# Hyena filter stage: last layer's weights as sum and difference, channel sums as columns with a small reciprocal, absolute sum as a maximum, one written order

## The chip, the core and the metric

The kernel runs on one core of a Trainium2 chip. The core has TensorE (PE, matrix products into PSUM), VectorE (DVE), ScalarE (ACT), GpSimd (POOL) and DMA queues that are issued by SyncE (SP). Each engine takes its instructions in one order and waits at semaphores for the others. The metric is the device time of one execution in microseconds; the time of a kernel is the median of its runs.

## The reference

Two blocks of a diffusion transformer work on 512 image tokens and 256 context tokens of width 1024. The first block's mixer is half a Fourier transform and half a Hyena operator: a convolution as long as the sequence, whose filter comes from a small network over positions. This is the part that the change rewrites:

```python
h = jnp.sin(f * (h @ w3 + b3))          # third sine layer
h = h @ w4                              # L x 1024
h_fwd = h[:, :512] * decay
h_bwd = h[:, 512:] * decay
two_sided = concatenate([h_fwd, zeros((1, 512)), h_bwd[:0:-1]])
two_sided = two_sided / sum(abs(two_sided), axis=0)
return rfft(two_sided, axis=0)
...
u_h = dwconv3(proj[..., 512:], conv_w, conv_b)
x0, x1, v = split(u_h, 3)
y_h = x0 * long_conv(v * x1, spectrum, hy_bias)
```

The first time step of h_bwd is left out of the filter (in its place stands the row of zeros). The division is by one absolute sum for each of the 512 channels. The filter is made for the image (512 steps) and for the context (256 steps).

## The kernel before

Products in this kernel are made of three: each fp32 operand is split into a rounded high half and the remainder, its low half, and high by high, low by high and high by low are added in PSUM (L149, L150, L151). For a weight this means a load of 512 KB into a buffer `wr`, the high half `wh` on ScalarE (L124) and the low half `wl` on VectorE (L129). There are three buffers each of `wr`, `wh` and `wl`, in rotation, and the rows of the modulation weights (`wmodT`, two products with `junk` at L241 on VectorE) pass through `wr` too. In the text such a row with its two products is a modulation row, and its products a modulation pair.

PSUM has three buffers `mm` of 1024 columns and two `ms` of 512. A result must leave its `mm` buffer before the third next product may start.

The mixer starts with the norm and projections 0 to 2, for which an order of PE, DVE, ACT and SP is written out by hand. With them run three sine layers of the filter's network; the last sine (L382 to L391 on VectorE, then L412 on ScalarE) makes `h3`. Then the filter stage follows, between about 72 and 156 us of the profile. In it:

- Six time tiles of 128 steps (4 and 5 for the context, 0 to 3 for the image): `filter_mm` (L421) makes forward and backward halves as a product of `h3` with `w4`. `filter_pm` multiplies both with the decay on VectorE (L430, L431), clears the first time step of the backward half, makes sum and difference on GpSimd (L437), their high halves on ScalarE, and the absolute sum of both halves with two ScalarE operations and one on GpSimd (L441 to L443). `filter_lo` makes the low halves.
- `filter_sum` (L459): the sum over time as a product with a 128 x 128 block of constants, so that each partition holds all 512 sums, and a reciprocal of 128 x 512 on VectorE (L461).
- `filter_spec`: a Fourier table `ftab` times the tiles, 12 products for each of the context's two tables, 24 for each of the image's four. `filter_scale` (L497 to L499) multiplies with the reciprocal and adds the skip row `brow`. `filter_nyquist` (L475 to L478) makes the one row of the highest frequency.
- Between them lie projections 3, 4 and 5. The last two go through `conv3`: one ScalarE operation (L371) and two on VectorE (L372, L373), which read the projection's PSUM buffer.

Behind the stage come projections 12, 8, 13, 9, 14, 10, 15 and 11 with their convolutions, folds and transposes (L695). In the filter stage and behind it the order on every engine is chosen by a scheduler, with the edges that `issue_after` adds.

Of the kernel before, what the change touches and what calls it, by code (L numbers as in the profile page):

```python
# [76 lines left out]
class Builder:  # L77
# [117 lines left out]

    def load_sb(self):
        nc = self.nc
        for j in range(2):
            nc.sync.dma_start(self.sb[:, j, :], self.I["cboth"][j : j + 1, :].partition_broadcast(P))
            nc.scalar.activation(self.sb[:, j, :], self.sb[:, j, :], AF.Silu)  # L200
# [223 lines left out]

    def filter_pm(self, ps, dec, first):

        nc, v = self.nc, self.nc.vector
        f = self.t(self.S2, [P, 512], F32, "s2")
        b = self.t(self.S2, [P, 512], F32, "s2")
        v.tensor_tensor(f, ps[:, 0:512], dec, op=ALU.mult)  # L430
        v.tensor_tensor(b, ps[:, 512:1024], dec, op=ALU.mult)  # L431
        if first:
            v.memset(b[0:1, :], 0.0)
        parts = []
        for tg, op in (("ap", ALU.add), ("am", ALU.subtract)):
            s = self.t(self.S2, [P, 512], F32, "s2")
            nc.gpsimd.tensor_tensor(s, f, b, op=op)  # L437
            hi = self.t(self.pg, [P, 512], F32R, tg + "h", 4)
            self.hi(hi, s)
            parts.append((s, hi))  # L440
        nc.scalar.activation(f, f, AF.Abs)  # L441
        nc.scalar.activation(b, b, AF.Abs)
        nc.gpsimd.tensor_tensor(f, f, b, op=ALU.add)  # L443
        return parts, f

    def filter_lo(self, parts):
        out = []
        for tg, (s, hi) in zip(("ap", "am"), parts):
            lo = self.t(self.pg, [P, 512], F32R, tg + "l", 4)
            self.lo(lo, s, hi)  # L450
            out.append((hi, lo))
        return out

    def filter_sum(self, sums, nhalf):

        ps = self.ms()
        on = self.onesN[nhalf]
        for i, f in enumerate(sums):
            self.nc.tensor.matmul(ps, on, f, start=i == 0, stop=i == len(sums) - 1)  # L459
        S = self.t(self.pf, [P, 512], F32, "S")  # L460
        self.nc.vector.reciprocal(S, ps)  # L461
        return S
# [45 lines left out]
    def mixer(self):  # L508
# [9 lines left out]
        for nh in (512.0, 256.0):  # L518
            self.onesN[nh] = self.t(self.pf, [P, P], F32, f"on{int(nh)}")
            v.memset(self.onesN[nh], nh)  # L520
# [1315 lines left out]
```

## Time and profile before

| | us |
|---|---|
| median of 3 runs | 1661.32 |
| lowest and highest run | 1657.84 and 1666.68 |
| the profiled execution | 1657.69 |
| its span, first to last instruction | 1655.9 |
| VectorE busy from 72 to 160 us with low halves of weights (L129, 12 of 128 x 1024 or 512) | 17.0 |
| VectorE busy there with modulation products (L241, 13) | 16.8 |
| VectorE busy there with the two wide reciprocals (L461) | 6.7 |

A line of a group in the profile names a line of the program, an engine, an operation, the tiles (out<-in) and a shape, then busy time, the mean of one and the idle time before it with what ended that. In a timeline the columns are the start in us, the duration, the engine, the line and the tiles; in brackets stands how long the engine sat idle before it, and who released it. Of stretches of the run (from:to) the busy time of each engine is given, in the order PE, weight loads (PEld), DVE, ACT, POOL, then the clock that was granted to TensorE (1.00 is full speed), the share of DMA and GB/s. The duration of a matmul overlaps the next one; its cost is from start to start.

### The profile page before, as it was taken

What the parts mean: (1) busy time and instruction counts of PE and PEld (TensorE: products, weight loads), DVE (VectorE), ACT (ScalarE), POOL (GpSimd) and SP (SyncE); (2) the same over time, 40 slices, a digit from 0 to 9 for tenths busy, and PEclk for the clock granted to TensorE, in tenths of its full rate; (3) what the DMA queues carried; (4) which work ended last, traced back from release to release, by engine and by line L of the source; (5) the groups of instructions that cost most, each with busy time, mean ns of one, the idle gap of its engine ahead of it and who ended that gap; (6) DMA issues with size and microseconds to landing.
All of it is one profiled execution on the core that took longest, in us unless ns stands there. A gap on an engine that the chain in (4) does not pass through costs nothing.

```text
span 1655.9 us, 20680 instructions
## 1 busy us (share of the span) xinstructions
PE 1588.1 (96%) x8178; PEld 1290.3 (78%) x8178; DVE 1057.4 (64%) x1695; ACT 617.4 (37%) x876; POOL 125.7 (8%) x177
## 2 busy tenths in 40 slices
PE   4989998999999999999998999999999999999999
PEld 2757787888888888888887887666659878878877
DVE  5698969967877354553444576899987544344243
ACT  4432224424222112222122245989864433133131
POOL 0152115000000000000000000222210000000000
PEclk9999999999999999999999999999999999999999
DMA  9325411432444133431430420000014222222222
GB/s 345 132 77 179 173 61 61 170 137 98 156 153 153 64 127 141 142 139 64 140 115 30 146 68 20 13 10 13 1 69 166 85 97 94 90 101 90 89 89 89
DMA packets 54540, 173.34 MB, mean 105 GB/s; under 512 B 6187, under 2 KB 9453, under 8 KB 53421
## 3 DMA queue, kind: packets, MB, share of 16 engines
q1 hardware_dynamic: 54445, 172.03, 29.3%
q8 instruction: 64, 1.05, 0.2%
q14 instruction: 31, 0.25, 0.0%
HBM read 166.24 MB, written 5.77 MB: 104 GB/s over the span
## 4 chain that ended last, share of the span: by engine, by line
PE 77%; DVE 14%; DMA 3%; POOL 2%; ACT 2%; issue 2%; SPq 0%; POOLq 0%; DVEq 0%; ACTq 0%
PE mm L149 23%; PE mm L151 23%; PE mm L150 23%; PE pv L1506 2%; DVE junk L241 2%; DVE wl L129 1%; DVE S L1482 1%; PE s L1452 1%; DMA wr<-wmodT 1%; POOL s L437 1%; DVE wr L1521 1%; PE k L149 1%; PE k L151 1%; PE k L150 1%; DVE mx L1466 0%
## 5 line engine op out<-in xcount | busy, mean ns | idle before, releaser
L149 PE MATMUL mm<-hh,wh 128*128 128x512 f32 (+2 forms) x1360 | 482.5, 358 | 10.6 <-DVE x L373 6.6
L151 PE MATMUL mm<-hh,wl 128*128 128x512 f32 (+2 forms) x1360 | 480.2, 354 | 1.6 <-DVE wl L129 1.6
L150 PE MATMUL mm<-hl,wh 128*128 128x512 f32 (+2 forms) x1360 | 480.3, 354 | 1.4 <-DVE hl L311 1.4
L124 ACT ACTIVATE wh<-wr 128x1024 fp32r<-128x1024 f32 (+2 forms) x192 | 197.6, 1032 | 584.5 <-PE mm L150 554.5
L129 DVE TENSOR_TENSOR wl<-wr,wh 128x1024 fp32r<-128x1024 f32 (+2 forms) x192 | 233.9, 1221 | 254.8 <-ACT wh L124 248.3
L149 PEld LDWEIGHTS mm<-hh,wh 128*128 128x128 f32 x1360 | 257.6, 190 | 58.8 <-issue 14.5
L150 PEld LDWEIGHTS mm<-hl,wh 128*128 128x128 f32 x1360 | 257.9, 190 | 39.5 <-DVE hl L311 2.5
L151 PEld LDWEIGHTS mm<-hh,wl 128*128 128x128 f32 x1360 | 258.0, 190 | 38.4 <-DVE wl L129 1.8
L241 DVE SCALAR_TENSOR_TENSOR junk<-wr,sb 128x1024 bf16<-128x1024 f32 x128 | 157.3, 1229 | 29.8 <-DMA wr<-wmodT 28.8
L151 PE MATMUL mm<-ah,wl 128*128 128x512 f32 (+1 forms) x480 | 172.3, 359 | 0.0
L150 PE MATMUL mm<-al,wh 128*128 128x512 f32 (+1 forms) x480 | 172.1, 359 | 0.0
L149 PE MATMUL mm<-ah,wh 128*128 128x512 f32 (+1 forms) x480 | 172.1, 359 | 0.0
L1048 DVE SCALAR_TENSOR_TENSOR xr<-mm,mod,xr 128x512 f32<-128x512 f32 (+1 forms) x100 | 61.8, 632 | 153.1 <-PE mm L151 152.7
L149 PEld LDWEIGHTS mm<-ah,wh 128*128 128x128 f32 x480 | 90.4, 188 | 14.7 <-issue 0.2
L150 PEld LDWEIGHTS mm<-al,wh 128*128 128x128 f32 x480 | 90.3, 188 | 14.6
L151 PEld LDWEIGHTS mm<-ah,wl 128*128 128x128 f32 x480 | 90.2, 188 | 14.4
L1506 PE MATMUL pv<-S,V 128*128 128x512 f32 x192 | 93.8, 597 | 2.6 <-ACT S L1485 2.6
L1072 ACT ACTIVATE fg<-fg 128x772 f32<-128x772 f32 (+1 forms) x44 | 32.6, 741 | 98.3 <-DVE fg L373 98.3
L1460 ACT ACTIVATE S<-s,rks 128x512 f32<-128x512 f32 x96 | 62.8, 686 | 12.0 <-PE pv L1506 8.0
L1506 PEld LDWEIGHTS pv<-S,V 128*128 128x128 f32 x192 | 34.4, 190 | 34.9 <-issue 29.4
L1478 POOL PARTITION_ALL_REDUCE mx<-mx x16 | 45.2, 2825 | 162.8 <-DVE mx L1475 162.8
L1482 DVE TENSOR_TENSOR S<-S,mx 128x1536 f32<-128x1536 f32 x32 | 55.3, 1749 | 2.3 <-POOL mx L1478 2.3
(330 smaller groups left out, 2266.1 us busy)
## 6 DMA issues: line engine op xcount, KB each, us to landing
wr<-w_up SPq DMA_DIRECT2D x88, 512.0 KB, 3.2
wr<-wmodT SPq DMA_DIRECT2D x80, 512.0 KB, 3.2
wr<-w_dn SPq DMA_DIRECT2D x32, 512.0 KB, 3.2
wm<-wmod0a SPq DMA_DIRECT2D x8, 1024.0 KB, 7.8
wr<-w_in SPq DMA_DIRECT2D x16, 512.0 KB, 3.2
wr<-w_out SPq DMA_DIRECT2D x13, 512.0 KB, 3.2
wr<-w_dn SPq DMA_DIRECT2D x17, 384.0 KB, 3.3
wr<-w_o SPq DMA_DIRECT2D x11, 512.0 KB, 3.2
```

Source lines behind the costliest of these rows:

```text
L124: self.nc.scalar.activation(dst, src, AF.Copy)
L129: (eng or self.nc.vector).tensor_tensor(dst, src, hi.bitcast(F32), op=ALU.subtract)
L149: mmul(out, wh, xh, start=start, stop=False)
L150: mmul(out, wh, xl, start=False, stop=False)
L151: mmul(out, wl, xh, start=False, stop=stop)
L241: nc.vector.scalar_tensor_tensor(junk, raw, 1.0, self.sb[:, j, :], op0=ALU.mult, op1=ALU.mult, accum_out=acc)
L1048: nc.vector.scalar_tensor_tensor(x[m][:, a2:b2], ps[:, a2:b2], mod[:, 8 * sec + m, c : c + 1], x[m][:, a2:b2], op0=ALU.mult, op1=ALU.add)
L1072: nc.scalar.activation(g[:, :n], g[:, :n], AF.Silu)
L1460: nc.scalar.activation(c.S[a][j // 3][:, j % 3, :], c.ps[a, j], AF.Copy, scale=c.r[:, g : g + 1])
L1478: nc.gpsimd.partition_all_reduce(c.m[a][:, 1, :], c.m[a][:, 0, :], P, bass.bass_isa.ReduceOp.max)
L1482: v.tensor_tensor(c.S[a][h], c.S[a][h], mb.to_broadcast([P, 3, T]), op=ALU.subtract)
L1506: nc.tensor.matmul(c.P[a], V[:, j, o : o + 128], c.S[a][j // 3][:, j % 3, :], start=j == 0, stop=j == 5)
```

## The change

The stage computes the same filter with other steps, and a written order takes the place of the scheduler's.

- `filter_w4` (new): the halves of `w4` are replaced by their sum and difference, with two GpSimd operations and a ScalarE copy, while projections 0 to 2 run. The product with `h3` then gives sum and difference at once, and `filter_pm` multiplies them with the decay. In the first time step both must be the forward half alone; it is the average of the two, so one VectorE operation and two on ScalarE work on one partition of tiles 0 and 4.
- The absolute sum |f| + |b| is the larger of |f + b| and |f - b|: two ScalarE operations and a maximum on VectorE. GpSimd has no part in it.
- `filter_sum`: the tile is now the stationary operand and a column of constants the moving one, so that the sums stand as columns (128 x 4 in all). Their reciprocal is taken of 128 x 4. `spread` broadcasts each column with a product against the identity, and ScalarE copies the result to SBUF.
- From the copies of projections 0 to 2 to the last table, PE, DVE, ACT and POOL take the order in which the program is written. Weights are loaded at other places, and nine modulation rows stand in the stage, where the program had three (the scheduler had drawn more of them forward).

```diff
+    def filter_w4(self):
+        f, b = self.w4[:, 0:512], self.w4[:, 512:1024]
+        t = self.t(self.S2, [P, 512], F32, "s2")
+        self.nc.gpsimd.tensor_tensor(t, f, b, op=ALU.add)
+        self.nc.gpsimd.tensor_tensor(b, f, b, op=ALU.subtract)
+        self.nc.scalar.copy(f, t)
...
+        for c in range(2):
+            v.tensor_tensor(s[c], ps[:, 512 * c : 512 * c + 512], dec, op=ALU.mult)
+        if first:
+            v.tensor_tensor(r[0:1, :], s[0][0:1, :], s[1][0:1, :], op=ALU.add)
+            for c in range(2):
+                self.nc.scalar.activation(s[c][0:1, :], r[0:1, :], AF.Copy, scale=0.5)
...
+        for c in range(2):
+            self.nc.scalar.activation(s[c], s[c], AF.Abs)
+        v.tensor_tensor(f, s[0], s[1], op=ALU.max)
...
-            self.nc.tensor.matmul(ps, on, f, start=i == 0, stop=i == len(sums) - 1)
-        self.nc.vector.reciprocal(S, ps)
+        for b in range(4):
+            for i, f in enumerate(sums):
+                self.nc.tensor.matmul(rt[:, b : b + 1], f[:, P * b : P * b + P], self.onesN[nhalf], start=i == 0, stop=i == len(sums) - 1)
+        self.nc.vector.reciprocal(c[:, 0:4], rt[:, 0:4])
+        def spread():
+            R = self.ms()
+            for b in range(4):
+                self.nc.tensor.matmul(R[:, P * b : P * b + P], c[:, b : b + 1].to_broadcast([P, P]), self.ident, start=True, stop=True)
+            self.nc.scalar.copy(S, R)
...
+            w3 = self.wload(I["w_in"][3])
             h3 = layer(2, layer(2, pa, 1), 2)
...
+        with self.tc.manual_schedule(engines={ENG.PE, ENG.DVE, ENG.Activation, ENG.Pool}):
...
+            p3 = proj(3, 0, w3)
+            a5, f5 = self.filter_lo(s5, h5)
+            tbc = [self.wsplit(w, 512) for w in tbc]
+            self.filter_skip(256.0)
+            for j in range(2):
+                nc.scalar.activation(self.sb[:, j, :], self.sb[:, j, :], AF.Silu)
+            gemvs(1)
+            mm_ = {0: self.filter_mm(h3, 0)}
+            spread_c = self.filter_sum([f4, f5], 256.0)
+            nc.scalar.copy(Uf[3], p3[:, :TW])
+            mm_[1] = self.filter_mm(h3, 1)
+            s0 = self.filter_pm(mm_[0], dec[0], True)
+            Sc = spread_c()
...
+            p4 = proj(4, 0, w4)
+            Hs[1] = self.filter_scale(sp1, Sc)
+            nyc = self.filter_nyquist(ac, Sc)
+            self.filter_skip(512.0)
+            gemvs(1)
+            mm_ = {tt: self.filter_mm(h3, tt) for tt in (2, 3)}
+            w5 = self.wload(I["w_in"][5])
+            conv(4, x0[0], p4)
...
+            p5 = proj(5, 0, w5)
+            a3, f3 = self.filter_lo(s3, h3_)
+            wx = self.wload(I["ftab"][0])
+            gemvs(1)
+            spread_x = self.filter_sum([f0, f1_, f2_, f3], 512.0)
+            for ft in range(4):
+                sp = self.filter_spec(ax, wx)
+                if ft == 0:
+                    S = spread_x()
+                    ny = self.filter_nyquist(ax, S)
+                    conv(5, x0[1], p5)
+                wx = self.wload(I["ftab"][ft + 1]) if ft < 3 else None
+                parts = self.filter_scale(sp, S)
...
+                gemvs(2 if ft else 0)
```

The order on VectorE at the start of the stage, before the change. The first row is the last low half of the norm, L382 to L391 are the last sine's operations, `wl_713` is the low half of projection 3's weights, and L430 the first filter product's decay:

```order
L311 SCALAR_TENSOR_TENSOR hl_111_349<-s_142_608,mod_4_73,hh_110_348 128x256
L466 TENSOR_SCALAR brow_117<-brow_117 128x512
L382 TENSOR_SCALAR s_143_651<-ms_603,pcol_67 128x384
L384 TENSOR_SCALAR s_144_653<-s_143_651 128x384
L385 TENSOR_SCALAR s_144_653<-s_144_653 128x384
L390 SCALAR_TENSOR_TENSOR s_143_651<-s_144_653,s_143_651 128x384 x3
L391 TENSOR_SCALAR s_143_651<-s_143_651 128x384
L129 TENSOR_TENSOR wl_713<-wr_710,wh_712 128x1024
```

The same place in the change, where the sine's operations are L376 to L385 and the low half is `wl_658`:

```order
L305 SCALAR_TENSOR_TENSOR hl_111_349<-s_142_609,mod_4_73,hh_110_348 128x256
L129 TENSOR_TENSOR wl_658<-wr_655,wh_657 128x1024
L376 TENSOR_SCALAR s_147_661<-ms_607,pcol_67 128x384
L378 TENSOR_SCALAR s_148_663<-s_147_661 128x384
L379 TENSOR_SCALAR s_148_663<-s_148_663 128x384
L384 SCALAR_TENSOR_TENSOR s_147_661<-s_148_663,s_147_661 128x384 x3
L385 TENSOR_SCALAR s_147_661<-s_147_661 128x384
L432 TENSOR_TENSOR s_163_706<-mm_700,s_91_318 128x512
```

The low half of projection 3's weights has moved from behind the sine to ahead of it, and the scaling of the skip row to a later place.

On VectorE, from the image's reciprocal to the low half of table 2, in the change. L491 and L492 are the Nyquist row, L366 and L367 the convolution of projection 5, `wl_1164` and `wl_1200` the low halves of tables 1 and 2, L511 and L513 the scaling:

```order
L466 RECIPROCAL fsum_1112<-ms_1095 128x4
L491 TENSOR_TENSOR s_260_1155<-ms_1146,S_1144 1x512
L492 TENSOR_TENSOR s_260_1155<-s_260_1155,brow_117 1x512
L366 SCALAR_TENSOR_TENSOR x_17_110<-mm_1022,pcol_67,x_17_110 128x771
L367 SCALAR_TENSOR_TENSOR x_17_110<-mm_1022,pcol_67,x_17_110 128x771
L129 TENSOR_TENSOR wl_1164<-wr_1161,wh_1163 128x1024
L511 TENSOR_TENSOR s_264_1167<-mm_1114,S_1144 128x512
L513 TENSOR_TENSOR s_265_1168<-mm_1114,S_1144 128x512
L129 TENSOR_TENSOR wl_1200<-wr_1197,wh_1199 128x1024
```

Before, the low halves of tables 1 and 2 (`wl_1143`, `wl_1181`) stood ahead of the convolution of projection 5 (L372, L373):

```order
L129 TENSOR_TENSOR wl_1143<-wr_1140,wh_1142 128x1024
L129 TENSOR_TENSOR apl_1002<-s_232_991,aph_993 128x512
L129 TENSOR_TENSOR aml_1004<-s_234_995,amh_997 128x512
L129 TENSOR_TENSOR wl_1181<-wr_1178,wh_1180 128x1024
L372 SCALAR_TENSOR_TENSOR x_17_110<-mm_1012,pcol_67,x_17_110 128x771
L461 RECIPROCAL S_1089<-ms_1084 128x512
L373 SCALAR_TENSOR_TENSOR x_17_110<-mm_1012,pcol_67,x_17_110 128x771
```

So each table's low half now stands behind the work on the table ahead of it.

On the DMA queue at the stage's end, before the change: `wr_1266` holds the weights of projection 12, the next stage's first, and `wr_1216` those of the last table.

```order
L137 DMA wr_1178<-ftab 128x1024
L137 DMA wr_1216<-ftab 128x1024
L137 DMA wr_1266<-w_in 128x1024
L237 DMA wr_1321<-wmodT 128x1024
L137 DMA wr_1334<-w_in 128x1024
L237 DMA wr_1389<-wmodT 128x1024
```

In the change `wr_1255` is the last table, `wr_1353` are the weights of projection 12, and these take the buffer of `wr_1278`:

```order
L137 DMA wr_1255<-ftab 128x1024
L733 DMA Hd_155_689<-s_270_1203 128x512
L733 DMA Hd_156_690<-s_271_1204 128x512
L231 DMA wr_1268<-wmodT 128x1024
L231 DMA wr_1278<-wmodT 128x1024
L231 DMA wr_1320<-wmodT 128x1024
L733 DMA Hd_157_691<-s_286_1261 128x512
L733 DMA Hd_158_692<-s_287_1262 128x512
L231 DMA wr_1330<-wmodT 128x1024
L137 DMA wr_1353<-w_in 128x1024
```

Four modulation rows now stand between the last table and projection 12.

More of the change, by code (lines that the diff above doesn't have):

```diff
@@ L194, in setup @@
         self.sb = self.t(self.sbp, [P, 2, D], F32, "sb")
[L196 to L200, printed above, removed]
     def gemv_raw(self, chunk):
@@ L640, in mixer @@
-        for g in range(3):
-            nc.scalar.copy(Uf[g], ps3[g][:, :TW])
-        with self.tc.issue_after(last.ins), self.tc.issue_after(last_act.ins):
-            tcs = [time_tile(4 + i) for i in range(2)]
-            nc.scalar.copy(Uf[3], proj(3)[:, :TW])
-            nc.sync.dma_start(self.brow, I["hyb"].partition_broadcast(P))
-            self.filter_skip(256.0)
-            tbc = [self.wload(I["ftab"][ft, :, 0:512], 512) for ft in range(2)]
-            self.load_sb()
-            for tt in range(4):
-                dec[tt] = tp()
-                nc.sync.dma_start(dec[tt], I["decay"][tt])
```

128 lines of the change are left out of this document (70 added, 58 removed).

## The prediction

> **What bounds the kernel now.** I read the page first, then TensorE's waits, then the filter stage in stretches, and last the single rows on which a term rests.
>
> ```profile
> PE 1588.1 (96%) x8178; PEld 1290.3 (78%) x8178; DVE 1057.4 (64%) x1695; ACT 617.4 (37%) x876; POOL 125.7 (8%) x177
> ...
> PE 77%; DVE 14%; DMA 3%; POOL 2%; ACT 2%; issue 2%; SPq 0%; POOLq 0%; DVEq 0%; ACTq 0%
> ```
>
> TensorE is busy for 96% and carries 77% of the chain that ends last. So the change is worth what it does to TensorE's idle time and to its work, in the filter stage that it rewrites. TensorE's waits between 60 and 240 us (total, times, longest):
>
> ```profile
> PE mm L149 <- DVE x L373: 6.6, 1, 6.6
> PE ms L459 <- POOL s L443: 3.0, 3, 1.8
> PE mm L695 <- ACT wh L124: 2.1, 1, 2.1
> PE mm L695 <- DVE tm L688: 1.8, 1, 1.8
> ```
>
> The first two are the filter stage's: projection 5 waits for VectorE to end the convolution of projection 4 (both need that PSUM buffer), and the channel sums wait for GpSimd's absolute sum. The last two are transposes of the next stage. In stretches (columns: TensorE, weight loads, VectorE, ScalarE, GpSimd, granted clock, DMA):
>
> ```profile
> 110.30:116.70 6.40, 0.00 (x0) 0.00 (x0) 5.82 (x10) 3.88 (x6) 3.07 (x2) 0.72 0.22 83
> 116.70:126.80 10.10, 10.06 (x49) 8.77 (x50) 6.86 (x9) 2.94 (x5) 7.68 (x5) 0.84 0.25 82
> 131.00:155.70 24.70, 24.70 (x106) 18.90 (x105) 22.52 (x31) 3.19 (x4) 3.87 (x3) 1.00 0.45 160
> ```
>
> After its 6.4 us of idling TensorE ran projection 5 at a granted clock of 0.84, which cost 10.1 x 0.16 = 1.6 us. The last 24.7 us, the four tables, have no idle time at all. All that can be won here is 6.6 + 3.0 + 1.6 = 11.2 us, 0.7% of the execution's 1657.69, if nothing new waits.
>
> **The start of the stage: +4.5 us.** The written order splits the weights of projection 3 ahead of the filter's last sine. The rows of before:
>
> ```profile
> 66.28 0.68 DVE L382 TENSOR_SCALAR s<-ms,pcol 128x384 f32<-128x384 f32 x1 [1.07 <-PE ms L408]
> 70.02 0.52 ACT L412 ACTIVATE s<-s 128x384 f32<-128x384 f32 x1 [4.61 <-DVE s L391]
> 70.45 1.04 ACT L124 ACTIVATE wh<-wr 128x1024 fp32r<-128x1024 f32 x1
> 71.52 1.23 DVE L129 TENSOR_TENSOR wl<-wr,wh 128x1024 fp32r<-128x1024 f32 x1 [1.60 <-ACT wh L124]
> 72.53 3.70 PE L421 MATMUL mm<-w,s 64*128 64x512 f32 x8
> ```
>
> The high half (70.45) cannot go earlier: three such buffers exist, and the oldest is read by projection 0 until about 70.4. VectorE takes its queue in order, so the sine's seven operations now stand behind the low half, which ends near 72.66. They keep their 3.74 us (66.28 to 70.02), so the sine starts at 76.4 and the first filter product at 77.0 instead of 72.53. TensorE has nothing queued ahead of that product but what ends at 72.6: **+4.5**, and a wait of 4.4 us where there was none.
>
> **Prices for the written order.**
>
> ```profile
> 107.14 1.99 PE L421 MATMUL mm<-w,s 64*128 64x512 f32 x8
> 109.06 1.12 PE L459 MATMUL ms<-s,on 128*128 128x512 f32 x2
> ...
> 117.17 1.22 DVE L129 TENSOR_TENSOR wl<-wr,wh 128x1024 fp32r<-128x1024 f32 x1
> 118.31 0.69 DVE L430 TENSOR_TENSOR s<-mm,s 128x512 f32<-128x512 f32 x1
> ...
> 137.01 0.40 PE L475 MATMUL ms<-aph,altr 128*1 128x512 f32 x1
> ...
> 138.87 0.39 PE L149 MATMUL mm<-aph,wh 128*128 128x512 f32 x1
> ...
> 144.49 0.40 PE L149 MATMUL mm<-aph,wh 128*128 128x512 f32 x1
> ...
> 147.76 1.21 DVE L241 SCALAR_TENSOR_TENSOR junk<-wr,sb 128x1024 bf16<-128x1024 f32 x1
> ...
> 150.44 0.68 DVE L497 TENSOR_TENSOR s<-mm,S 128x512 f32<-128x512 f32 x1
> 151.04 0.68 DVE L499 TENSOR_TENSOR s<-mm,S 128x512 f32<-128x512 f32 x1
> ...
> 177.50 1.02 DVE L372 SCALAR_TENSOR_TENSOR tm<-mm,pcol,tm 128x771 f32<-128x771 f32 x1
> 178.56 1.02 DVE L373 SCALAR_TENSOR_TENSOR tm<-mm,pcol,tm 128x771 f32<-128x771 f32 x1
> ```
>
> ```profile
> wr<-w_in SPq DMA_DIRECT2D x16, 512.0 KB, 3.2
> ```
>
> From start to start: a pair of modulation products takes VectorE 2.68 us (147.76 to 150.44), a 512-wide operation 0.6, a convolution's two operations 2.1 (177.50 to 178.56, and 1.02), a low half 1.14 (117.17 to 118.31). TensorE takes 1.9 for the image filter's eight Nyquist products (137.01 to 138.87; 0.9 for the context's four), 5.6 for a table (to 144.49), 1.9 for the filter products of time tiles 2 and 3 (107.14 to 109.06). A weight load lands after 3.2 us and its high half takes ScalarE 1.05.
>
> **Projection 5: 5.7 instead of 6.6, -0.9.** Behind projection 4 TensorE does 0.9 Nyquist and 1.9 filter products, 2.9 in all. VectorE meanwhile must wait for the Nyquist (0.9), then do two Nyquist operations and the skip row's scaling (1.8), a modulation pair (2.7), a low half (1.1) and the convolution (2.1): 8.6. The old wait stays.
>
> **Table 1: +4.1.** Its low half now stands behind the Nyquist's two operations (1.3), projection 5's convolution (2.1) and itself (1.14), with the hand-overs 4.6 us after TensorE's Nyquist. TensorE can do two of the table's products first (0.5). Before, nothing waited here.
>
> **Table 3: +1.6.** Its low half stands behind table 1's scaling (1.2), two modulation pairs (5.4) and itself (1.14): 7.7 after table 1 ends, against 5.6 + 0.5 of work.
>
> **Projection 12, the next stage's first: +6.9.** Its weights take the buffer that the fourth modulation row after table 0 gives back, and that row's pair stands behind table 3's low half, table 2's scaling (1.2) and another pair. So the buffer comes free 1.2 + 2.7 + 2.7 = 6.6 after that low half; 3.2 of load and 1.05 of high half make 10.8. Table 3 itself is done after 5.2, so TensorE waits 5.6. The low half stands behind table 3's scaling and one and a half more pairs, and costs 1.3 more. Before, these weights were issued ahead of the modulation rows and landed during table 1.
>
> **Sums: -3.0 and +0.8.** The wait for GpSimd goes whole, since the maximum is one 0.6 us operation of VectorE with a projection between it and the sum's product. The wide reciprocal goes too, but it hid behind tables. TensorE's work:
>
> ```profile
> L461 DVE RECIPROCAL S<-ms x2: 3342/3347/3352, 90.2 to 132.3; 128x512 f32<-128x512 f32 x2
> ```
>
> ```profile
> 17.59 0.15 DVE L283 TENSOR_SCALAR nrm_s<-ms 128x4 f32<-128x4 f32 x1
> ...
> 48.79 0.95 PE L224 MATMUL ms<-cst,s 128*128 128x2 f32 x8
> 49.60 0.48 PE L149 MATMUL mm<-hh,wh 128*128 128x512 f32 x1
> ...
> 126.74 1.88 PE L459 MATMUL ms<-s,on 128*128 128x512 f32 x4
> ```
>
> Six products of 0.94 (1.88 for two) become 24 narrow ones of 0.2 (four in 0.81, 48.79 to 49.60) and two spreads of four products, taken at the same 0.8: 5.6 to 6.4. A reciprocal of 128x4 is in no row. Its bounds are 0.15 (an operation of that shape) and 3.35 (the wide one); I take 0.15, nearest in shape. At 3.35 the context's spread would come at most 1.5 later, behind a filter product, and the image's would still hide behind a table.
>
> **Costed at nothing.** These rows are the cover:
>
> ```profile
> 50.00:70.00 20.00, 19.14 (x114) 15.09 (x113) 12.70 (x27) 6.91 (x11) 0.00 (x0) 1.00 0.00 1
> ...
> 63.41 2.00 ACT L200 ACTIVATE sb<-sb 128x1024 f32<-128x1024 f32 x2
> ```
>
> The sum and difference of the filter weights are two GpSimd operations and a ScalarE copy, done while GpSimd has no row and ScalarE works for 6.9 of 20 us; the first projections' products hide them. Without that slack the copy would cost its 0.6. The conditioning's two Silu (2.0 us) move from 63 us to behind the filter's absolute values, ahead of the copy of projection 3, which TensorE needs only for table 0 and after two more filter products and the sum, 5.2 us (1.8 each and 1.6); without these they would cost 2.0. The row-0 average and its two copies: between 0.15 (the short row) and 0.6 each, I take 0.6, hidden by projection 3. The loads of decay, skip row and conditioning keep their places on the DMA queue. GpSimd's removed sums were off TensorE's path but for the 3.0 above.
>
> **The clock: +4.** Four waits of over 4 us (4.4, 5.7, 4.1 and 5.6) replace one. Each can halve the clock behind it, as also this wait of 2.65 us did:
>
> ```profile
> 259.50:262.10 2.60, 0.01 (x1) 0.00 (x0) 2.60 (x6) 1.27 (x4) 2.60 (x3) 1.00 0.12 20
> 262.10:266.00 3.90, 3.37 (x20) 3.24 (x20) 3.90 (x7) 1.02 (x2) 0.95 (x1) 0.65 0.24 63
> 266.00:270.00 4.00, 4.00 (x16) 3.71 (x16) 2.34 (x5) 1.37 (x3) 2.54 (x2) 0.50 0.16 58
> ```
>
> Behind it TensorE lost 3.9 x 0.35 + 4.0 x 0.5 = 3.4 us; behind the 6.4 us wait, 1.6. Three more such waits cost 4.8 to 10; part falls on table 2, where TensorE has 1.6 to wait anyway. I take 4, and keep 0 and 10.
>
> The Trainium skill ("TensorE: Matmul & The Clock Gate", "What's actually happening") says that the clock halves after an idle window of about 3.4 us, free-running. By it the wait of 2.65 us should have left the clock alone; the 0.50 behind it says otherwise, and the trace decides. By that rule all four waits here are long enough to cool, with a loss of about 1.7 us each, an estimate from that page: 5.1 instead of 4.
>
> **Given back: -4.** The next stage's two waits (2.1 and 1.8) came from its own weights and folds running late behind modulation rows; in the new order of loads the weights of projection 10 come earlier and the first fold 1.3 sooner against its transposes. I take -3 of 3.9. Six more modulation rows are done in the filter stage, so six fewer stand in the output projection, where TensorE waits little: -1, between 0 and -2.4.
>
> **The sum.** +4.5 - 0.9 + 4.1 + 1.6 + 6.9 - 3.0 + 0.8 + 4 - 4 = **+14.0 us**. The profiled execution took 1657.69 us: **1671.7**. It lies 3.6 us under the median of the three runs shown (1661.32) and beside the lowest (1657.84), so the range reaches further up than down. A measurement of this kernel can tell about 0.5%, 8.3 us, from no change.
>
> **Rivals.** *VectorE is faster than these rows, and the result is no slower (0.22).* GpSimd slows it: with GpSimd at work the same operation took 1.10 us, and 0.69 without.
>
> ```profile
> 104.12 1.10 DVE L129 TENSOR_TENSOR apl<-s,aph 128x512 fp32r<-128x512 f32 x1 [1.25 <-ACT aph L124]
> ...
> 105.38 0.69 DVE L129 TENSOR_TENSOR aml<-s,amh 128x512 fp32r<-128x512 f32 x1 [0.15 <-ACT amh L124]
> ```
>
> GpSimd falls almost silent here. Place: the three queues behind projection 4, table 0 and table 1. They decide: if VectorE's 8.6 behind projection 4 falls under TensorE's 2.9, and the others likewise, 11.4 of waits go: 1660.3, within 0.5%. Against it: my prices are mostly rows with GpSimd idle already, and the order itself, not the load, makes these waits.
>
> *The new stage runs as TensorE's work alone (0.04).* No wait but the first: 4.5 - 6.6 - 3.0 + 0.8 - 1.6 = -5.9, with up to 3 from later: 1649 to 1652. It needs projection 12's weights early, and the order of loads says the opposite. Even this is hardly more than 0.5%.
>
> *The waits run longer (0.22).* Behind projection 12, 13 modulation rows remain where 10 did, 3 x 2.7 = 8 us more for an engine busy for 19.0 of 20 us at 180 to 200 us:
>
> ```profile
> 180.00:200.00 20.00, 18.23 (x106) 15.81 (x105) 19.00 (x36) 4.70 (x5) 2.88 (x3) 1.00 0.43 151
> ```
>
> With half or all of that exposed, or with the wait at 259.5's loss of 3.4 behind each of the three more waits (10 for 4): 1678 to 1684.
>
> **How the numbers follow.** The forecast, 1664 to 1678, has 0.52; the longer waits 0.22; no slower 0.22; TensorE's work alone 0.04. Slower by over 0.5% is 0.52 + 0.22 = 0.74, within it 0.22, faster 0.04. The range 1660 to 1684 takes in the ends of the clock's term and leaves out TensorE's work alone, a third of the no-slower case and the far end of the longer waits.
>
> **What would show it.** TensorE's first filter product near 77 behind a wait on the sine; waits of about 5.7, 4.1 and 5.6 on the convolution, table 1's low half and projection 12's high half; the granted clock at 0.5 behind them; no wait on GpSimd; a reciprocal of under 0.3. I am wrong if tables 1 to 3 run without a gap, or if projection 12 starts before 160 us.

## The result, and the profile after

The changed kernel took **1686.37 us** (median of 4 runs, 1683.87 to 1689.75); the kernel before took 1659.58 beside it. The ratio is 1.0164, 95% interval 1.0139 to 1.0189: slower by 1.6%, some 27 us, where the prediction said 14.0. The direction was right, and the time lies above the range (1660 to 1684).

The profiled execution took 1689.75 us, with a span of 1687.6. Its page shows TensorE's busy time grown by 21.6 us, though its work hardly grew:

```profile
PE 1609.7 (95%) x8230; PEld 1308.3 (78%) x8230; DVE 1050.6 (62%) x1701; ACT 621.7 (37%) x883; POOL 99.8 (6%) x161
...
PE 80%; DVE 14%; issue 2%; ACT 2%; POOL 1%; DMA 1%; SPq 0%; POOLq 0%; ACTq 0%; DVEq 0%
```

VectorE and GpSimd have less to do than before, as the change intends. More instructions can't make 21.6 us (52 rows were added); the same products took longer on average. TensorE's waits between 60 and 240 us (total, times, longest):

```profile
PE mm L151 <- DVE wl L129: 7.3, 3, 3.3
PE mm L149 <- ACT wh L124: 6.7, 2, 6.0
PE mm L149 <- DVE x L367: 6.0, 1, 6.0
PE mm L415 <- ACT s L406: 4.4, 1, 4.4
```

These are the predicted waits, at the predicted places: 4.4 behind the sine, 6.0 behind the convolution, the rest behind halves of weights. No wait on GpSimd is left. The rows of TensorE's timeline that place them (in brackets the wait; the third and fourth stand in table 1, the fifth in table 3):

```profile
81.19 3.78 PE L415 MATMUL mm<-w,s 64*128 64x512 f32 x4 [4.39 <-ACT s L406]
...
132.94 0.77 PE L149 MATMUL mm<-hh,wh 128*128 128x512 f32 x1 [6.00 <-DVE x L367]
...
157.11 0.50 PE L149 MATMUL mm<-aph,wh 128*128 128x512 f32 x1 [0.67 <-ACT wh L124]
...
161.11 0.79 PE L151 MATMUL mm<-aph,wl 128*128 128x512 f32 x1 [3.27 <-DVE wl L129]
...
177.53 0.50 PE L151 MATMUL mm<-aph,wl 128*128 128x512 f32 x1 [2.51 <-DVE wl L129]
...
188.94 0.79 PE L149 MATMUL mm<-hh,wh 128*128 128x512 f32 x1 [6.00 <-ACT wh L124]
191.71 0.80 PE L151 MATMUL mm<-hh,wl 128*128 128x512 f32 x1 [1.55 <-DVE wl L129]
```

The filter stage (first filter product to projection 12), before, in the view of stretches (TensorE, weight loads, VectorE, ScalarE, GpSimd, granted clock, DMA share, GB/s):

```profile
72.50:155.70 83.20, 73.62 (x313) 52.77 (x313) 71.65 (x92) 26.58 (x40) 36.02 (x23) 0.96 0.35 124
```

And in the changed kernel, first the whole stage, then the stretches in which the clock was halved:

```profile
81.20:188.90 107.70, 89.29 (x364) 65.74 (x364) 67.57 (x110) 29.75 (x44) 7.70 (x6) 0.83 0.26 93
...
81.10:91.30 10.20, 10.12 (x17) 5.01 (x18) 4.46 (x7) 3.94 (x9) 0.00 (x0) 0.50 0.16 56
...
101.60:111.80 10.20, 10.20 (x27) 6.86 (x27) 4.11 (x7) 4.54 (x8) 0.00 (x0) 0.50 0.01 6
...
132.90:135.80 2.90, 2.86 (x8) 2.48 (x9) 2.90 (x6) 2.38 (x4) 0.00 (x0) 0.51 0.41 151
142.60:146.00 3.40, 3.40 (x33) 3.40 (x32) 1.92 (x6) 0.00 (x0) 0.00 (x0) 1.00 0.60 214
146.00:149.40 3.40, 3.40 (x11) 2.82 (x11) 0.18 (x1) 0.00 (x0) 0.00 (x0) 0.50 0.24 94
...
159.60:166.40 6.80, 5.29 (x13) 4.13 (x14) 4.56 (x5) 0.00 (x0) 1.28 (x1) 0.50 0.37 135
...
186.90:197.20 10.30, 6.71 (x19) 5.28 (x20) 9.80 (x20) 2.11 (x2) 0.00 (x0) 0.50 0.87 293
```

The stage's clock fell from 0.96 to 0.83. In clock time (the length of a stretch times the missing share of the clock) the stage lost 83.2 x 0.04 = 3.3 us before and 107.7 x 0.17 = 18.3 now. (Some 2 us of either fall on idle time at half clock, which costs nothing twice.) Four of the half-clock stretches stand behind waits or begin in them; two (from 101.6 and from 146.0) have no wait ahead of them. TensorE's rows there:

```profile
100.28 2.38 PE L464 MATMUL ms<-on,s 128*128 128x1 f32 x16
102.59 1.22 PE L415 MATMUL mm<-w,s 64*128 64x512 f32 x1
...
142.78 3.89 PE L464 MATMUL ms<-on,s 128*128 128x1 f32 x32
146.53 0.77 PE L149 MATMUL mm<-aph,wh 128*128 128x512 f32 x1
```

From 142.8 to 146.0 TensorE did nothing but products that stream one column, without a gap, at a clock of 1.00; at 146.0 the clock was halved.

**Where the 33.2 us stand** by which projection 12 starts later (155.7 to 188.94). The sum of waits ahead of it grew by 13.3 (24.4 less the 1.55 that falls behind its start, against 9.6). Clock time grew by 15.0. The stage itself began late in this execution: its first product is at 81.19, of which 4.4 is the wait, and 4.2 came from ahead of the stage. There TensorE's products ran at half pace until about 47 us (the trace has no record of the clock before 47 us and prints 1.00). The rows of the same eight products show it, first in the changed kernel, then in another (section 6, projection 12), which has the same program up to there and its first filter product at 77.20:

```profile
29.33 1.87 PE L218 MATMUL ms<-cst,s 128*128 128x2 f32 x8 [0.71 <-ACT s L213]
```

```profile
29.01 1.05 PE L218 MATMUL ms<-cst,s 128*128 128x2 f32 x8 [0.71 <-ACT s L213]
```

This is a difference between executions, as the programs are the same up to there; this execution was also the highest of its four, 3.4 over the median. 13.3 + 15.0 + 4.2 = 32.5, which leaves 0.7 for TensorE's added work.

In the next stage the kernel did not catch up. Its last transposes start 38.1 later than before, so it lost another 4.8 (kernel before, then the changed kernel):

```profile
236.24 0.49 PE L795 MATMUL mm<-cst,tm 128*128 128x128 f32 x3
```

```profile
274.30 0.38 PE L856 MATMUL mm<-cst,tm 128*128 128x128 f32 x2
```

The two waits of before (1.77 and 2.07) have become one there, with a half clock behind it:

```profile
257.19 0.98 PE L756 MATMUL mm<-cst,tm 128*128 128x128 f32 x6 [2.15 <-DVE tm L749]
```

```profile
258.64:262.05 3.41, 3.41 (x12) 2.94 (x12) 3.00 (x4) 0.37 (x1) 0.00 (x0) 0.50 0.41 154
```

### The profile page after: what moved, and what is told of

Same layout as the page of the kernel before. It is cut to its first block, busy times and chain, and to the rows that moved or that the text cites. A ratio compares the mean times of both kernels' runs of the same rounds, so it can differ in the third digit from the quotient of the medians.

```text
span 1687.6 us, 20778 instructions
## 1 busy us (share of the span) xinstructions
PE 1609.7 (95%) x8230; PEld 1308.3 (78%) x8230; DVE 1050.6 (62%) x1701; ACT 621.7 (37%) x883; POOL 99.8 (6%) x161
## 4 chain that ended last, share of the span: by engine, by line
PE 80%; DVE 14%; issue 2%; ACT 2%; POOL 1%; DMA 1%; SPq 0%; POOLq 0%; ACTq 0%; DVEq 0%
PE mm L149 23%; PE mm L151 23%; PE mm L150 23%; PE pv L1567 2%; DVE junk L235 2%; DVE S L1543 1%; DVE wl L129 1%; PE s L1513 1%; DVE wr L1582 1%; PE mm L415 1%; PE ms L210 1%; PE k L149 1%; PE k L150 1%; DVE hl L305 1%; PE k L151 1%
```

## The experiments

The waits were as predicted, so the theory to be tested was: **the clock costs three to four times what was forecast**, because each wait is followed by a long stretch at half clock, and because narrow products halve it too, without a wait. The rivals: the written order costs time in a way that the waits don't show; the new steps are slower in any order; the coolings at the sums come from waits near them.

### 1. The waits, filled with work

```diff
+        def fill(n):
+            ps = self.ms()
+            for _ in range(n):
+                nc.tensor.matmul(ps, hh[0][:, 0:P], hl[0][:, 0:512], start=True, stop=True)
...
+            fill(16)
             mm_ = {tt: self.filter_mm(h3, tt) for tt in (4, 5)}
...
+            fill(24)
             p5 = proj(5, 0, w5)
...
+                if ft in (1, 3):
+                    fill(14 if ft == 1 else 10)
                 sp = self.filter_spec(ax, wx)
...
                 gemvs(2 if ft else 0)
+            fill(24)
```

> The changed kernel with its five waits filled: 88 products of 128x512 that nobody reads stand ahead of the first filter product (16), projection 5 (24), tables 1 (14) and 3 (10) and projection 12 (24), a little less than each wait has room for. The waits keep their length, but TensorE works in them. Theory A (waits cool the clock and this is most of the error): the half-clock stretches behind these waits go, those behind the narrow sums stay, and the time falls by 5 to 12 us against the changed kernel although TensorE has 20 us more work. Theory B (the clock isn't what the waits cost): no change, or longer.

Measured: **1672.90 us**, ratio 1.0079 (1.0063 to 1.0094): 13.5 us less than the changed kernel's median, or 14 by the ratios, with 88 more products. The stage from its first filter product on, in five stretches (the second and the fourth lie behind the two narrow sums):

```profile
76.00:91.80 15.80, 15.80 (x73) 11.15 (x73) 10.77 (x18) 9.13 (x15) 0.00 (x0) 0.98 0.23 80
91.80:102.00 10.20, 10.20 (x27) 6.83 (x27) 4.72 (x10) 4.74 (x8) 0.00 (x0) 0.52 0.23 84
102.00:136.20 34.20, 34.00 (x184) 27.52 (x184) 24.92 (x41) 10.28 (x16) 2.60 (x2) 0.99 0.21 68
136.20:139.60 3.40, 3.40 (x10) 2.66 (x10) 0.00 (x0) 0.00 (x0) 0.00 (x0) 0.57 0.23 93
139.60:168.90 29.30, 28.17 (x124) 21.50 (x123) 21.14 (x32) 4.44 (x5) 3.86 (x3) 1.00 0.37 126
```

The half clock behind every filled wait is gone; what is left stands behind the two narrow sums. VectorE, ScalarE and the loads had the same work in the same order. So about 13.5 of the 27 us were not the waits but the clock behind them. This is theory A, a little beyond its 12.

### 2. The new algebra alone, a clean stage

The kernel before with `filter_w4`, the new `filter_pm`, `filter_hi` and `filter_lo` only:

```diff
         def time_tile(tt):
-            pm, f = self.filter_pm(self.filter_mm(h3, tt), dec[tt], tt in (0, 4))
-            return self.filter_lo(pm), f
+            s = self.filter_pm(self.filter_mm(h3, tt), dec[tt], tt in (0, 4))
+            return self.filter_lo(s, self.filter_hi(s))
```

> The kernel before with only the sum and difference of the filter weights and the maximum; wide sums, scheduler's order. If the prediction's term for GpSimd's sums holds, the waits of 3.0 us for GpSimd go and nothing else grows: 1 to 4 us less than before. The rival: the scheduler's order shifts and a wait on another engine takes their place, or the first wait on the sine (6.4 us in the scheduler-ordered run of the changed steps) is made by this part: no change or up to 5 us more.

Measured: 1650.83 us, ratio **0.9931** (0.9908 to 0.9954). It is more than expected, since in this order the wait on the convolution went as well as those for GpSimd. The stage and its only wait:

```profile
76.70:150.30 73.60, 73.41 (x314) 52.11 (x314) 65.64 (x98) 29.53 (x44) 6.36 (x5) 1.00 0.43 140
```

```profile
PE mm L421 <- DVE s L510: 0.2, 1, 0.2
```

73.6 us instead of 83.2, without a wait worth the name and without a half clock: a stage in which one thing can be changed at a time. The next two runs do that.

### 3. One wait put into the clean stage

```diff
+            w3 = self.wload(I["w_in"][3])
             h3 = layer(2, layer(2, pa, 1), 2)
...
-            nc.scalar.copy(Uf[3], proj(3)[:, :TW])
+            nc.scalar.copy(Uf[3], proj(3, 0, w3)[:, :TW])
```

> The sum, difference and maximum alone, with one wait put into the clean stage: projection 3's weights are split ahead of the last sine, as in the changed kernel. Theory A (a wait of over 4 us costs itself and the cooling behind it, three windows of 3.4 us at half clock): first filter product 4.4 us later, then about 10 us of half clock, so 4.4 + 3 to 5 = 7.5 to 9.5 us more than without. Theory B (the wait alone): 4 to 5 us more.

Measured: 1660.88 us, ratio 1.0004 (0.9991 to 1.0017), so 10 us more than without (12 by the ratios), for a wait of 5.3:

```profile
81.02 7.19 PE L421 MATMUL mm<-w,s 64*128 64x512 f32 x8 [5.35 <-ACT s L412]
```

```profile
80.30:94.00 13.70, 12.98 (x27) 7.51 (x28) 10.45 (x22) 4.54 (x9) 0.00 (x0) 0.52 0.51 167
```

Theory A, with a stretch even longer than expected: 13.7 us at half clock (79.75 to 93.40 in the clock's record), TensorE at work in the last 12.4 of them, which cost 6.2 us. The stage as a whole is only 4.4 longer than in section 2 (78.0 against 73.6), for the scheduler also put two groups of filter products side by side that stood apart there (eight rows in 1.99 us at 119.73, against 1.98 for each four). The four filter products, 64 rows deep, took 7.2 us here and 3.7 in the kernel before. One wait of 5.3 us took back the whole gain of the algebra.

### 4. Column sums in the clean stage, one column wide and 128 wide

The clean stage with the change's `filter_sum` and `spread`; and the same with a block of 128 equal columns as the moving operand:

```diff
-                self.nc.tensor.matmul(rt[:, b : b + 1], f[:, P * b : P * b + P], self.onesN[nhalf], start=i == 0, stop=i == len(sums) - 1)
+                self.nc.tensor.matmul(rt[:, P * b : P * b + P], f[:, P * b : P * b + P], self.onesN[nhalf], start=i == 0, stop=i == len(sums) - 1)
-        self.nc.vector.reciprocal(c[:, 0:4], rt[:, 0:4])
+        self.nc.vector.reciprocal(c[:, 0:4], rt.rearrange("p (b c) -> p b c", c=P)[:, :, 0])
```

One column:

> The sum, difference and maximum alone (whose filter stage ran for 73.5 us without a wait or a half clock) plus the column sums, scheduler's order. Theory A (products of one column cool the clock with no wait near): half clock behind each of the two sums, 3 to 14 us of it in the stage, and a stage 3 to 8 us longer. Theory B (the cooling in the changed kernel comes from waits): the clock stays at 1.00 and the stage grows by under 2 us.

128 columns:

> The run with sum, difference, maximum and column sums, but each of the 24 sum products streams a block of 128 equal columns instead of one (the reciprocal reads the first of each block), so that the instructions, their order and the spread stay and only the width changes. Theory A (it is the narrow stream that counts as idle): no half clock behind the sums; by the wide sum's price of 0.94 for 512 columns each product takes about 0.25 to 0.35 us, 24 of them 6 to 8 us, against 5 for the narrow ones. Theory B (the cooling comes from the many switches of the stationary operand or the spread): half clock as with one column.

Measured: 1644.64 us, ratio **0.9907** (0.9891 to 0.9924) with one column; 1643.77, 0.9914 (0.9885 to 0.9942) with 128. Both are faster than either kernel. For the clock the image's sum is the test. With one column (a product of fp32 stands as two rows, so 26 rows are 13 products; then the stretches):

```profile
119.57 3.23 PE L470 MATMUL ms<-on,s 128*128 128x1 f32 x26
```

```profile
119.50:122.10 2.60, 2.60 (x25) 2.55 (x24) 0.49 (x1) 0.38 (x1) 0.00 (x0) 1.00 0.00 0
122.10:125.50 3.40, 3.40 (x12) 2.92 (x13) 2.22 (x3) 0.00 (x0) 0.00 (x0) 0.50 0.00 0
```

With 128:

```profile
119.20 3.06 PE L470 MATMUL ms<-on,s 128*128 128x128 f32 x26
```

```profile
119.20:122.10 2.90, 2.90 (x28) 2.90 (x26) 2.38 (x3) 1.33 (x2) 0.00 (x0) 1.00 0.12 16
122.10:125.50 3.40, 3.40 (x21) 2.76 (x20) 2.19 (x5) 0.59 (x1) 0.00 (x0) 1.00 0.38 141
```

The same 26 rows at the same place take the same time at full clock, with the same spread behind them: 0.11 us from row to row with 128 columns (119.20 to 122.02), 0.12 with one, where the last 0.56 us already ran at half clock. So a product of 128 columns took 0.22, just under the 0.25 to 0.35 that I gave it, and no more than one of one column. Behind one column the clock was halved for 3.4 us, behind 128 it stayed at 1.00. It is the narrow stream that counts as idleness to the clock. One rival is chance: within a run the clock changes only at points 3.41 us apart (36.77, 40.19, 122.11 and 125.52 with one column; 34.16, 40.99, 194.59 and 198.00 with 128), and these points lie elsewhere in every execution. But the piece between two such points that ended at 122.11 held 2.53 us of the sum with one column, and the piece from 119.49 to 122.91 held 2.53 us of the sum with 128 columns. Theory A's size was too high, though: only one stretch followed, 1.7 us lost, and the stage grew by 2.7 (76.3 us against 73.6, and against 74.8 with 128 columns), not 3 to 8. The context's sum (16 rows, two of them ahead of a table) cooled nothing.

### 5. Wide sums in the written order

The changed kernel with the old `filter_sum`.

> The changed kernel with the old channel sums (128x128 block of constants, 512 sums in every partition, wide reciprocal) in the same written order. Theory A (products that stream a single column count as little activity, so the clock cools behind the narrow sums although TensorE never waits): the half-clock stretches at 101.6 to 111.8 us and at 146 to 149.4 us vanish, 5 to 7 us less than the changed kernel, though the wide reciprocals add 6.4 us to VectorE's queue and may lengthen the waits for table 1 and projection 5 by up to 3. Theory B (these coolings come from the waits of VectorE ahead of them): they stay, and the kernel is the same or up to 5 us slower.

Measured: 1688.15 us, ratio 1.0183 (1.0161 to 1.0205), not to be told from the changed kernel. The stretches around the context's sum, where the changed kernel was at half clock, and the stage:

```profile
94.30:101.60 7.30, 7.30 (x20) 3.26 (x20) 4.60 (x5) 0.80 (x1) 0.00 (x0) 1.00 0.47 168
101.60:111.80 10.20, 8.93 (x43) 6.85 (x42) 7.40 (x13) 5.42 (x9) 0.48 (x1) 1.00 0.16 51
...
77.50:178.20 100.70, 80.66 (x313) 55.71 (x313) 73.98 (x110) 28.78 (x42) 7.70 (x6) 0.89 0.30 100
```

The cooling at the sum went, and the stage of the profiled execution was 7.0 us shorter, as theory A said; the time of the runs didn't follow. For the clock this decides, for the time it doesn't. In the changed kernel the piece between two points of the clock ahead of this half clock (98.22 to 101.63) held 1.35 us of one-column products and 1.91 of products with 64 rows; in the clean stage 1.15 us of a narrow sum among products of 128 rows cooled nothing. So the products with 64 rows may have a part in this cooling, which no run here separates.

### 6. Single steps undone in the written order

Projection 3's weights loaded early, but split behind the sine:

```diff
-            w3 = self.wload(I["w_in"][3])
+            w3 = self.wraw(I["w_in"][3])
...
+            w3 = self.wsplit(w3)
             mm_ = {tt: self.filter_mm(h3, tt) for tt in (4, 5)}
```

> The changed kernel with one step put back: projection 3's weights are loaded early, but split into halves only behind the filter's last sine. Theory A (the clock was mis-sized: the first wait cools TensorE's clock and the K=64 filter product behind it keeps it cool for three windows): the wait of 4.4 us goes and with it the half-clock stretch from 81 to 91 us, so 4.4 + about 4 = 8 to 9 us less than the changed kernel (ratio to before about 1.011). Theory B (the clock term was right, the time came from elsewhere): only the wait goes, 4 to 5 us less (ratio about 1.0135).

Measured: 1675.60 us, ratio 1.0111 (1.0091 to 1.0131), theory A's figure: 8.8 us by the ratios for a wait of 4.4. The first filter product starts without a wait, and takes its old time:

```profile
72.73 3.70 PE L415 MATMUL mm<-w,s 64*128 64x512 f32 x8
```

Projection 12's weights ahead of the last modulation rows:

```diff
-                wx = self.wload(I["ftab"][ft + 1]) if ft < 3 else None
+                wx = self.wload(I["ftab"][ft + 1] if ft < 3 else I["w_in"][12])
...
-            hconv(12 + i, cv, 1 if i < 3 else 2)
+            hconv(12 + i, cv, 1 if i < 3 else 2, wx if i == 0 else None)
```

> The changed kernel with projection 12's weights taken ahead of the last modulation rows of the stage (as the table ahead of them), nothing else. The wait of 6.0 + 1.6 us ahead of projection 12 goes. Theory A (each such wait costs its length and the half clock that follows): also the half-clock stretch of 186.9 to 197.2 us goes, 7 + 5 = 12 us less than the changed kernel, about 1674. Theory B (a wait costs its length): 6 to 8 us less, about 1679. Theory C (the modulation rows, which only move, then hold up the next stage): less than 5 us.

Measured: 1685.03 us, ratio 1.0141 (1.0113 to 1.0169): less than 4 us under the changed kernel, within the error, so theory C rather than A. The waits (60 to 300 us) show it: the one of 6.0 on `wh` went, others on `wl` came.

```profile
PE mm L151 <- DVE wl L129: 10.9, 6, 3.3
```

This row has 7.8 in the changed kernel over the same time. VectorE had the same modulation rows to do, and TensorE met them at other places.

### 7. The order

The changed kernel's steps, with the order left to the scheduler (the early split of projection 3's weights included):

```diff
-        with self.tc.manual_schedule(engines={ENG.PE, ENG.DVE, ENG.Activation, ENG.Pool}):
+        with ExitStack():
```

> The changed kernel's new steps (sum and difference, maximum, column sums), but the order in the stage left to the scheduler. Theory A (the written order makes the waits of 5.7 to 6.0, 4.1 and 6.9 us): those waits go or shrink to under 3 us each, the stage ends 10 to 20 us earlier, and the time lies between the kernel before and 10 us above it; the half clock behind the narrow sums stays. Theory B (the new steps themselves are slower, for any order): no more than 5 us less than the changed kernel.

Measured: 1669.98 us, ratio 1.0073 (1.0053 to 1.0094), some 15 us less than in the written order, 2 us outside theory A. The wait on the convolution fell to 2.3 and those on weights to 0.6 us, while that on the sine grew:

```profile
PE mm L415 <- ACT s L406: 6.4, 1, 6.4
...
PE mm L149 <- DVE x L367: 2.3, 1, 2.3
...
PE mm L151 <- DVE wl L129: 0.6, 2, 0.4
```

The written order with its five waits taken out (the two edits of section 6, and these), once with column sums and once with the old wide ones:

```diff
             Hs[1] = self.filter_scale(sp1, Sc)
+            w5 = self.wload(I["w_in"][5])
+            conv(4, x0[0], p4)
             nyc = self.filter_nyquist(ac, Sc)
...
-            w5 = self.wload(I["w_in"][5])
-            conv(4, x0[0], p4)
...
                 sp = self.filter_spec(ax, wx)
+                wx = self.wload(I["ftab"][ft + 1] if ft < 3 else I["w_in"][12])
...
-                wx = self.wload(I["ftab"][ft + 1]) if ft < 3 else None
...
-                gemvs(2 if ft else 0)
+                gemvs(1 if ft else 0)
```

Columns:

> The changed kernel's steps with column sums, in a written order with its five waits taken out: projection 3's weights split behind the sine; projection 4's convolution and projection 5's weights ahead of the Nyquist row and the modulation rows; each next table's weights split ahead of the scaling of the one before; one modulation row behind a table instead of two; projection 12's weights with the last table. If the order makes the waits, TensorE's idle time in the stage falls from 23 to under 5 us and the stage (first filter product to projection 12) from 108 to 75 to 80 us: about 1650 to 1657. Theory A (narrow sums cool the clock by themselves): two half-clock stretches of 3.4 us or more remain behind the sums, though TensorE never waits there. Theory B (only waits cool it): the clock stays at 1.00 in the whole stage.

Wide:

> The same repaired order with the old wide sums. Theory A (narrow sums cool the clock): no half clock in the stage, 3 to 7 us under the repaired order with columns: 1645 to 1652, and so under the kernel before by 0.5%. Theory B: within 2 us of the repaired order with columns, or slower, by the wide reciprocals' 6.4 us on VectorE.

Measured: 1657.72 us, ratio 0.9983 (0.9970 to 0.9997) and 1656.13, 0.9979 (0.9960 to 0.9997). The stage of the first, then of the second:

```profile
72.50:157.70 85.20, 81.52 (x365) 62.40 (x365) 60.67 (x94) 31.28 (x46) 6.44 (x5) 0.90 0.28 93
```

```profile
71.40:148.90 77.50, 73.15 (x313) 51.10 (x313) 66.67 (x94) 30.32 (x44) 6.47 (x5) 1.00 0.31 102
```

Five edits of the order, with the new steps kept, brought back all that the change had lost. With columns the clock was 0.90 in the stage, with wide sums 1.00, so again the narrow sums cool it (two stretches, as theory A said; a wait of 2.3 us ahead of one of them helped). Of the 7.7 us between the stages only 1.6 arrived in the time, though, so theory A's times (1645 to 1652 with wide sums) were missed, and with columns the stage was 5 us longer than expected. What takes the gain back behind the stage was not tried.

### 8. Column sums in the kernel before

> The kernel before with one part of the change alone: channel sums as columns with the 128x4 reciprocal and the spread. Theory A (one-column products cool the clock): a half-clock stretch of 3 to 7 us behind each of the two sums, where the kernel before ran at full speed or nearly so; the time is 3 to 7 us longer than before, less up to 3 from the smaller reciprocal. Theory B (narrow products are only short work): TensorE's work +0.8, no new half-clock stretch, within 2 us of before.

The edit is that of section 4 (one column), made to the kernel before. Measured: 1662.49 us, ratio 1.0027 (1.0004 to 1.0051), 4.5 us more, in theory A's band. It doesn't decide: the waits for GpSimd's absolute sum grew in this order, and one of them was 5.0 us long, longer than the 4.4 us that was followed by half clock in the changed kernel.

```profile
PE ms L459 <- POOL s L443: 9.1, 4, 5.0
```

## Why the prediction was off

- **Start of the stage, +4.5:** right; the wait was 4.39. The first filter product, foreseen near 77, stood at 77.20 in section 6's second run and at 81.19 in this execution, for the half pace ahead of the stage.
- **Projection 5, 5.7:** right; 6.0, on the convolution.
- **Table 1, +4.1:** right; 0.67 on the high half and 3.27 on the low one, 3.94.
- **Table 3, +1.6:** 2.51, 0.9 more. **Projection 12, +6.9:** 6.0 + 1.55 = 7.55.
- **Sums, -3.0 and +0.8:** the waits for GpSimd went; but the added work is about 1.2 by the rows, not 0.8 (24 products of 0.22 and two spreads of 0.8, less 5.6); the 0.7 left over in the sum of the 33.2 is a remainder within its rounding. The reciprocal took 0.18, as the lower bound of 0.15 said:

```profile
102.70 0.18 DVE L466 RECIPROCAL fsum<-ms 128x4 f32<-128x4 f32 x1 [3.45 <-PE ms L464]
```

Together the prediction had 13.2 for these waits (4.5 - 0.9 + 4.1 + 1.6 + 6.9 - 3.0), and the trace has 14.8 (24.4 - 9.6).

- **The clock, +4: this step failed, by its size.** The stage alone lost 15.0 us more clock time than before, and the bounds of 0 and 10 didn't hold it. Two things were wrong in it. First, the price of the waits. "Three more such waits cost 4.8 to 10" took 1.6 to 3.4 for each, from the only two waits of before that showed a cooling, and of these 4 was taken, as part was to fall on table 2; but the half clock behind table 1's wait ended at 166.48, and table 2 begins at 168.77. Half of the time that TensorE worked in the half-clock stretches behind the waits is 5.1 us behind the first, 1.4 at projection 5, 2.6 at table 1 and 3.4 at projection 12 (behind the stage's end), 12.5 together; the wait at table 3 cooled nothing. Filling the waits measured 13.5. With the 1.6 of before taken off, 11 to 12 us are new, where the upper bound was 10. Second, the sums were priced by TensorE's work alone; that 2 to 4 us of one-column products count as idle time was no term at all. In the changed kernel their two stretches (10.2 and 3.4 us) cost 6.8 us of clock time in the trace. How much of that reaches the time isn't settled: taking them out did not shorten the runs of the written order, brought 1.6 us in the repaired order, and in the clean stage one column and 128 give the same time.

  Why one wait cost more than another can be read from the points, 3.41 us apart, at which the clock changes (in the changed kernel 81.15, 84.56, 87.98, 91.39 and so on). At projection 5 TensorE ran products of 128 rows from 132.94, and the clock was back at the next point, 135.76; at table 1, from 161.11, it was back at the second, 166.48. Behind the first wait products of 64 rows ran until 88.4, and it came back at the third point behind that wait's end, 91.39; in section 3 they ran until 88.1, and it came back at 93.40. At projection 12 a second wait of 1.55 fell into the second piece, and it came back at 197.20, the end of the third. The prediction asked only whether a wait cools, not what stands behind it. That the products of 64 rows themselves keep the clock low was not tried.
- **Given back, -4: wrong in sum.** By the next stage's last transposes 4.8 more was lost. About 1.7 of the two waits did come back (3.84 against 2.15), but the half clock behind the one that is left took 1.7 again, and the 1.55 us of waiting behind the stage's end and half of the 6.71 us that TensorE worked between 186.9 and 197.2, 3.4, come on top. At the end of the span the difference is 31.7 us; the medians differ by 26.8, as the profiled execution before lay 1.9 under its median and this one 3.4 over. What shrank 38.1 to 31.7 behind the next stage was not tried.
- **The rivals.** That every wait is cooled was named ("10 for 4", 1678 to 1684), and it came closest; its price per wait was still too low. That VectorE without GpSimd beside it runs its queues in time was rightly doubted for this order: the waits of the three queues stayed. But it is what happens in the scheduler's order, where the algebra alone takes 0.7% off.

In sum: terms that came from rows of the same operations (13.2 of waits, 0.8 of work) hit within 2 us; the one taken from two neighbouring cases was off by 11, and the one for what is given back by 9. By the Trainium skill ("TensorE: Matmul & The Clock Gate", "What's actually happening") the clock halves after an idle window of about 3.4 us; by it, as an estimate from that page, each wait would have lost about 1.7. The lengths of these stretches, 3.4, 6.8 and 10.2 us, agree with windows of that size; but behind the first wait three of them followed, so that estimate from the Trainium skill is a third of what that wait cost in clock (5.1).

## What to carry to other kernels

A wait that a written order puts into a dense TensorE stage can cost itself and once more its own length in clock (8.8 us for 4.4, 10 for 5.3); before one is accepted, its cooling is to be counted by what stands behind it (here 3.4 to 6.8 us of half clock where products of 128 rows stood there, 10 to 14 where products of 64 did), and where it can't be removed, work that nobody reads may pay (here 13.5 us). A chain of one-column products can be idleness to the clock (here 2.5 us of it in a piece of 3.4): 128 columns take the same time here. Test a bundle of edits one by one: here the algebra with column sums, in the scheduler's order, is faster by 0.9%, and the written order around it cost 2.6%.

## What the hardware showed unexpectedly

- Behind 2.5 us of fp32 products of one column, back to back, the clock was halved (13 of them, 119.57 to 122.66); behind 13 of 128 columns in the same place it was not, and they took no longer (3.23 and 3.06 us for the 26 rows).
- A wait of 5.3 us went with 13.7 us at half clock although TensorE was busy for the last 12.4 of them. The first 7.2 of these were products with 64 rows; that this is why the clock stayed low was not tried by itself.
- 88 products that nobody reads made a kernel 13.5 us faster.
- In each of these traces the clock changes only at points 3.41 us apart, and where these points lie differs between executions; a wait of 2.51 us in table 3 cooled nothing, one of 2.15 in the next stage did.
